# A two-layer encoder step in hi/lo-split fp32: the seven-product pair of token tiles also in layer 0, its passes re-ordered

## The chip, the cores and the metric

The kernel runs on one core of one Trainium2 chip. The metric is device time in microseconds (us) of one execution. Three executions of the kernel before took 2142.72 to 2146.37 us, median 2143.95. One further execution was recorded by the hardware profiler; all rows of the profile come from that one. Engines are called as in the profile: PE (TensorE, matmul), DVE (VectorE), ACT (ScalarE), POOL (GpSimd), SP (SyncE, which issues most DMAs).

## The reference, cut to what matters

1056 token rows (1024 of a prompt, 32 of a running stream), D = 1024 channels, two layers. Each layer is a mixer (layer 0: gated unit; layer 1: pooling over windows of 2, 4, 8 and 16 rows) and an FFN with 4096 hidden channels, with a norm before and behind each, and scales and shifts ("modulation") that come from a condition vector through w_ada.

```
for i in range(DEPTH):                                  # DEPTH = 2
    mod = jax.nn.silu(c) @ w_ada[i] + b_ada[i]
    sh1, sc1, gt1, sh2, sc2, gt2 = jnp.split(mod[:, None, :], N_MOD, axis=-1)
    h = rmsnorm(x, g_norm[i, 0]) * (1 + sc1) + sh1
    ...                                                 # mix: sgu_mixer (i = 0), pool_mixer (i = 1)
    x = x + gt1 * rmsnorm(mix, g_norm[i, 1])
    h = rmsnorm(x, g_norm[i, 2]) * (1 + sc2) + sh2
    f = jnp.square(jax.nn.relu(h @ ffn_w_up[i])) @ ffn_w_down[i]
    x = x + gt2 * rmsnorm(f, g_norm[i, 3])
```

All of it is in fp32. The two FFNs are most of the arithmetic.

## The kernel before, in words

**Tiles and number format.** Channels lie on the 128 partitions, tokens along the free axis. Three token tiles are kept in SBUF throughout: tiles 0 and 1 with 384 columns, tile 2 with 256 prompt and 32 stream columns, 288. `acc[t]` holds a tile's running sum, `hh[t]` and `hl[t]` the normed and modulated input of the next product, split into a high part (fp32r) and the rest. A product of fp32 operands is three matmuls (`products`, L1029 to L1031): high weight by high input, high weight by low input, low weight by high input, for each 128 channels of the contraction. Weights arrive in pieces of 512 KB, 1024 columns; ACT copies the high part (L534 in `do_w`), DVE subtracts it for the low part. All DVE rows of the profile carry L80, the line of the helper that records them, so they are told apart by tile names.

**Slots.** 16 slots of 1024 columns hold split weights, two for a piece. Four of them, the "ring" (tag R), are lent to other uses from a certain point on: when the piece `LEND_AT` is split, `w_call` takes the ring slots out of the turn, and what was the ring becomes room for the block sums below.

**FFN passes.** The FFN of a layer is cut into 8 chunks of 512 hidden channels. A pass is (layer, chunk, tiles): its eight pieces of weights (4 `up`, 4 `dn`) are loaded and split once and used by each of its tiles. The list `passes` (L374 to L381) gives the order on PE and of the weights. Layer 0 before: chunks 0 and 1 of tile 0, of tile 1, of tile 2; chunks 2 and 3 each with all three tiles; then chunks 4 to 7 of tile 0, of tile 1, of tile 2. Layer 1: chunks 0 to 3 of tile 0, of tile 1, then chunks 4 to 7 as pairs (below), then the eight of tile 2.

**A tile's pass** (`ffn_item`, L1453): four `up` products of 8 x 3 matmuls into PSUM (`pf`), ReLU and square on ACT, split into `fh` and `fl`, then `down`: eight products `pg` of 4 x 3 matmuls, each added to `acc` by DVE. `down` is put off (`pending`) and issued by `flush` (L1284) behind the next pass's first `up` product, so that PE has work while the hidden values are split.

**A pair pass** (`pair_item`, L1509, layer 1 chunks 4 to 7 before) takes tiles 0 and 1 at once. The two halves of the contraction (four blocks of 128 each, `HK`), two pieces of weights and two tiles make a 2 x 2 block product, done in seven block products of 12 matmuls where the plain form has eight. For that, DVE sums weight blocks (`quads`, L493, in four steps that take 2, 1, 2 and 2 slots) and sums of the input (`combos`, L1699; block sums `combo[1]` to `combo[4]`; the first of them, which overwrites half of tile 1's `hh` and `hl`, in `first_combo`, L1735). Results are combined by DVE (`r12`, `r22`, `r11`) and copied by ACT (`a1`, `b1`, `a2`, `a3`); the first PSUM tiles are `pfa` and `pfb`, with rows at L1542 to L1544. `paired` (L1919) starts `first_combo` ahead of the first pair pass.

**What sets the order of DVE and ACT work.** Each engine runs its own queue in the order in which the program issues. The program issues PE's work in order of `passes`, and after each product calls `weave` (L806), which advances two things: the stream of weight pieces and w_ada pieces (`stream`, in the order in which they are loaded; `some_ada`, L418 to L424, says how many w_ada pieces go behind a pass's weights, each of which gives DVE multiply-adds `aa`), and the `fillers`, generators that hold a tile's work between mixer and FFN. A filler advances while the program's own count of DVE time is below that of PE time. `finish(tag)` (L817) forces what is left of a filler. `run_ffn` (L1903) forces the filler of a tile ahead of its chunk 0, after a `flush`. `stream_ready` (L707) holds a piece back until its slots are free.

**The fillers around the FFNs.** `mix_to_ffn` (L1666): norm of the mixer's result and residual (`residual`, L916: for each channel block a scalar-tensor-tensor on `acc`, an addition of the kept input `xo_r`), the square sums on PE, then `modulate` (L957) and `apply` (L963): for each block a scalar-tensor-tensor on `acc`, an ACT activation into `hh`, a scalar-tensor-tensor into `hl`. `to_pool` (L1760), behind the last `down` of a tile in layer 0: the same residual, a norm, the pooling windows (`win1p..`), the small products with `pool_w_grp`, then `mix_to_ffn` for layer 1. In layer 1 tile 2's `apply` is kept in `late_norm` and made a filler only within the last pair pass.

Of the kernel before, what the change touches and what calls it, by code (L numbers as in the profile page):

```python
# [9 lines left out]
F32 = mybir.dt.float32  # L10
# [25 lines left out]
def tile_stream_encoder_step(  # L36
# [391 lines left out]
    for _, key, _, _ in [s for s in stream if s[0] == "two"]:  # L428
        for x in ("A1", "A22", "S12", "S34"):
            wpos[("up", key[1], key[2] // 2, x)] = wpos[key]  # L430
# [62 lines left out]
    def quads(n, j, r1, r2):  # L493

        a11, a12, a21, a22 = r1[:, :512], r1[:, 512:], r2[:, :512], r2[:, 512:]
        key = lambda x: ("up", n, j // 2, x)
        s3 = []

        def first():
            s3.append(work.tile([P, 512], F32, tag="aa", bufs=2, name=f"s3_{n}_{j}"))  # L500
            tt(out=s3[0], in0=a11, in1=a21, op=ALU.subtract)
            w_split(key("A1"), r1)

        def second():
            tt(out=a21, in0=a21, in1=a22, op=ALU.add)
            w_split(key("A22"), a22, 512)

        def third():
            tt(out=a22, in0=a21, in1=a11, op=ALU.subtract)
            w_split(key("S12"), r2)  # L510

        def fourth():
            tt(out=a12, in0=a12, in1=a22, op=ALU.subtract)
            state["raw"] -= 1
            wh, wl = w_pair(key("S34"))
            for at, x in ((0, s3[0]), (512, a12)):
                w = slice(at, at + 512)
                act(out=wh[:, w], in_=x, func=AF.Copy)
                tt(out=wl[:, w], in0=x, in1=wh[:, w].bitcast(F32), op=ALU.subtract)
            state["raw"] -= 1  # L520

        subs.extend([(2, first), (1, second), (2, third), (2, fourth)])

# [391 lines left out]

    def residual(st, l, cf, tag, out, store=True, stat=True, loads=None):  # L916
        t = st.t
# [8 lines left out]

        got = []
        yield from st.finish(got)
        r = got[0]
        st2 = Stat(t, tag + "x")  # L930
# [577 lines left out]

    def pair_item(p, after):  # L1509
        l, c, tiles = passes[p]  # L1510
# [45 lines left out]
        def up(jp):  # L1556
            name = f"{l}_{c}_{jp}"
            j = 2 * jp

            def done(key):  # L1560
                w_finish(("up", p, jp, key))

            pa, pb = ps_ms(f"pfa{name}"), ps_up(f"pfb{name}")
            quad_product(pa, jp, ("A1", 0), -11, True)
            a1 = copy(pa, f"a1{name}")
            weave()
            if jp == 0:
                flush()
                finish("combos")
            quad_product(pb, jp, ("S12", 0), 1, True)  # L1570
            b1 = copy(pb, f"b1{name}")
            weave()
            quad_product(pa, jp, ("S12", 512), 2, False)
            done("S12")
            a2 = copy(pa, f"a2{name}")
            weave()
            quad_product(pb, jp, ("S34", 512), -22, False)
            keep(1, j, add(a2, pb, f"r12{name}"))
            weave()
            quad_product(pa, jp, ("S34", 0), 3, False)  # L1580
            done("S34")
            a3 = copy(pa, f"a3{name}")
            keep(1, j + 1, add(a3, b1, f"r22{name}"))
# [4 lines left out]
            keep(0, j, add(a1, pc, f"r11{name}"))  # L1588
            weave()
            quad_product(pa, jp, ("A22", 0), 4, False)  # L1590
            done("A22")
            keep(0, j + 1, t_m(f"r21{name}"), pa[:, :n])
            weave()

        def down():
            sts = {}
            for q in range(4):
                wh, wl = need_w(("dn", p, q))
                for t in reversed(tiles):
                    for d in (2 * q, 2 * q + 1):  # L1600
                        ps = ps_dn(f"pg{l}_{c}_{t}_{d}")
                        terms = []
                        for j in (0, 1, 3, 2) if t == 1 else range(4):
# [9 lines left out]
                        if d % 2 == 1 and t == tiles[0]:  # L1613
                            w_finish(("dn", p, q))
                        weave(d % 2)
            for t in tiles if after is not None else ():
                after(sts[t])

        up(0)
        up(1)  # L1620
        if after is not None:
            fillers.append(late_norm.pop())
# [43 lines left out]
    def mix_to_ffn(st, l):  # L1666
        t = st.t
        out = []
        need_ada(l, 2)
        yield from residual(st, l, 1, f"r1_{l}_{t}", out, store=l == 0 or t < NT - 1)  # L1670
        if l == 1 and t == NT - 1:
# [10 lines left out]

    late_norm = []
    combo = {}
    HK = KB // 2
# [13 lines left out]
    def combos():  # L1699

        while lent["left"]:
            yield 1.0
        units = []
        for tag, n in (("R", 5), ("hh2", 3), ("hl2", 3)):
# [8 lines left out]
        for i in (2, 3, 4):  # L1713
            combo[i] = units[4 * i - 8 : 4 * i - 4]
        combo[1] = [(hh[1][:, k], hl[1][:, k]) for k in range(HK)]
        for k in (0, 2):
            x, y, z = (t_two(f"combo_{v}{k}") for v in "xyz")
            tt(out=x, in0=both(1, k)[0], in1=both(1, k)[1], op=ALU.add)
            tt(out=y, in0=both(1, HK + k)[0], in1=both(1, HK + k)[1], op=ALU.add)
# [4 lines left out]
            tt(out=z, in0=both(0, k)[0], in1=both(0, k)[1], op=ALU.add)  # L1724
            tt(out=x, in0=x, in1=z, op=ALU.subtract)
            yield True
# [3 lines left out]
            tt(out=z, in0=both(0, HK + k)[0], in1=both(0, HK + k)[1], op=ALU.add)  # L1730
            tt(out=z, in0=z, in1=y, op=ALU.subtract)
            keep_parts(z, combo[4][k : k + 2])
            yield False

    def first_combo():  # L1735

        for k in (0, 2):
            x, z = (t_two(f"combo1_{v}{k}") for v in "xz")
            tt(out=x, in0=both(1, k)[0], in1=both(1, k)[1], op=ALU.add)
            tt(out=z, in0=both(0, k)[0], in1=both(0, k)[1], op=ALU.add)  # L1740
            yield True
            tt(out=x, in0=x, in1=z, op=ALU.subtract)
            keep_parts(x, combo[1][k : k + 2])
            yield False
# [158 lines left out]
    def run_ffn(l, after):  # L1903
        for p, (pl, c, tiles) in enumerate(passes):
            if pl != l:
                continue
            if tiles == PAIR:
                if p > 0 and passes[p - 1][2] != PAIR:
                    paired()
                pair_item(p, after if c == 7 else None)  # L1910
                continue
            for t in tiles:
                if c == 0:
                    if any(f[0] == f"ffn{l}_{t}" for f in fillers):
                        flush()
                    finish(f"ffn{l}_{t}")
                ffn_item(p, t, after if c == 7 else None)

    def paired():  # L1919

        def stages():
            yield from first_combo()

        fillers.append(("combos", stages()))

# [157 lines left out]
```

## Time and profile before

| | |
|---|---|
| median of three executions | 2143.95 us (2142.72 to 2146.37) |
| profiled execution, its own time | 2141.37 us |
| its span (first to last instruction) | 2139.6 us |
| PE busy | 99% of the span |
| DVE, ACT, POOL busy | 71%, 48%, 1% |
| DMA | 320 MB moved, 150 GB/s on average |

How to read it: the page gives for each engine the busy time as a share of the span, and the same in 40 slices of 53.5 us each. Matmuls are pipelined and the length of one matmul in the profile includes the overlap with its neighbours, so what PE needs for a stretch is taken from counts over a window, not from the mean length. A group of rows such as `pg L1031` stands for all instructions from one line that write tiles of one name. A wait "A <- B: 1.2" says that the engine stood idle for 1.2 us and that B ended last of what it waited for.

### The profile page before, as it was taken

How to read it: one execution, taken by the hardware profiler on the slowest of the kernel's cores; microseconds unless marked ns; L12 is line 12 of the kernel's file. 1: busy time of each engine (PE TensorE's matmuls, PEld its weight loads, DVE VectorE, ACT ScalarE, POOL GpSimd, SP SyncE). 2: the span in 40 equal slices, each digit the busy share in tenths (PEclk: the TensorE clock that was granted, in tenths of full speed). 3: DMA queues.
4: the chain of work that ended last, by engine and by line, in shares of the span. 5: the costliest groups of instructions: out<-in, count | busy, mean ns of one | idle time of the engine just before them, and what ended most of it. 6: DMA issues, size and time to landing. Idle time of an engine off the chain costs nothing. (4 is left out here: it accounts for less than half of the span.)

```text
span 2139.6 us, 33156 instructions
## 1 busy us (share of the span) xinstructions
PE 2119.9 (99%) x13026; PEld 2054.6 (96%) x13026; DVE 1521.5 (71%) x2688; ACT 1018.0 (48%) x1743; POOL 22.3 (1%) x44
## 2 busy tenths in 40 slices
PE   8999999999999999999999999999999999999998
PEld 6878999999999999999999999999999999999998
DVE  6778838467778548486747879878879854569464
ACT  5634432234456652323445566666555543365454
POOL 0000000000000000000000000000000000001100
PEclk9999999999999999999999999999999999999999
DMA  8586524353447444243645465665545221138672
GB/s 291 163 263 210 182 83 137 94 154 101 138 129 219 128 150 146 86 141 110 191 128 160 145 183 174 188 189 153 175 136 154 83 76 60 59 115 231 171 206 82
DMA packets 401905, 320.18 MB, mean 150 GB/s; under 512 B 47406, under 2 KB 365142, under 8 KB 401748
## 3 DMA queue, kind: packets, MB, share of 16 engines
q1 hardware_dynamic: 400820, 316.77, 48.9%
q8 instruction: 102, 1.67, 0.3%
q0 software_dynamic: 896, 1.28, 0.2%
q14 instruction: 55, 0.45, 0.1%
q10 hardware_dynamic: 32, 0.01, 0.0%
HBM read 287.34 MB, written 30.66 MB: 149 GB/s over the span
## 5 line engine op out<-in xcount | busy, mean ns | idle before, releaser
L1029 PE MATMUL pg<-fh,wh_dn 128*128 128x384 f32 (+1 forms) x1240 | 397.8, 321 | 0.1
L1031 PE MATMUL pg<-fh,wl_dn 128*128 128x384 f32 (+1 forms) x1240 | 395.8, 319 | 1.2 <-DVE wl_dn L80 1.2
L1030 PE MATMUL pg<-fl,wh_dn 128*128 128x384 f32 (+1 forms) x1240 | 396.0, 319 | 0.0
L1029 PE MATMUL pf<-hh,wh_up 128*128 128x384 f32 (+1 forms) x1000 | 318.1, 318 | 0.0
L1031 PE MATMUL pf<-hh,wl_up 128*128 128x384 f32 (+1 forms) x1000 | 316.6, 317 | 0.1
L1030 PE MATMUL pf<-hl,wh_up 128*128 128x384 f32 (+1 forms) x1000 | 316.7, 317 | 0.0
L80 DVE TENSOR_TENSOR acc<-acc,pg 128x384 f32<-128x384 f32 (+1 forms) x336 | 174.1, 519 | 106.5 <-PE pg L1031 105.8
L1029 PEld LDWEIGHTS pg<-fh,wh_dn 128*128 128x128 f32 x1240 | 232.7, 188 | 1.9 <-ACT fh L1289 1.4
L1031 PEld LDWEIGHTS pg<-fh,wl_dn 128*128 128x128 f32 x1240 | 232.7, 188 | 1.4 <-DVE wl_dn L80 1.4
L1030 PEld LDWEIGHTS pg<-fl,wh_dn 128*128 128x128 f32 x1240 | 232.8, 188 | 0.6
L80 DVE TENSOR_TENSOR wl_dn<-raw,wh_dn 128x1024 fp32r<-128x1024 f32 x139 | 170.1, 1224 | 78.4 <-ACT wh_dn L534 67.9
L534 ACT ACTIVATE wh_dn<-raw 128x1024 fp32r<-128x1024 f32 x139 | 146.8, 1058 | 162.9 <-PE pg L1030 122.4
L80 DVE SCALAR_TENSOR_TENSOR aa<-raw,csil,aa 128x512 f32<-128x512 f32 (+1 forms) x364 | 204.5, 623 | 4.9 <-DMA raw<-in_w_ada_dram 4.7
L80 DVE TENSOR_TENSOR wl_up<-raw,wh_up 128x1024 fp32r<-128x1024 f32 x113 | 138.3, 1225 | 76.8 <-ACT wh_up L534 76.6
L1031 PEld LDWEIGHTS pf<-hh,wl_up 128*128 128x128 f32 x1000 | 188.0, 188 | 0.8 <-DVE wl_up L80 0.8
L1029 PEld LDWEIGHTS pf<-hh,wh_up 128*128 128x128 f32 x1000 | 187.6, 188 | 0.6 <-ACT wh_up L534 0.2
L1030 PEld LDWEIGHTS pf<-hl,wh_up 128*128 128x128 f32 x1000 | 187.7, 188 | 0.3
L534 ACT ACTIVATE wh_up<-raw 128x1024 fp32r<-128x1024 f32 x113 | 119.7, 1060 | 115.7 <-PE pf L1030 61.8
L534 ACT ACTIVATE ring<-raw 128x1024 fp32r<-128x1024 f32 x68 | 72.0, 1059 | 154.8 <-PE pf L1030 72.0
L1465 ACT ACTIVATE r<-pf 128x384 f32<-128x384 f32 (+1 forms) x160 | 71.2, 445 | 126.6 <-PE pf L1031 123.8
L80 DVE TENSOR_TENSOR fl<-r,fh 128x384 fp32r<-128x384 f32 (+1 forms) x180 | 93.5, 521 | 50.8 <-ACT fh L1289 50.1
L80 DVE TENSOR_TENSOR ring<-raw,ring 128x1024 fp32r<-128x1024 f32 x69 | 84.2, 1222 | 44.2 <-ACT ring L534 44.2
(403 smaller groups left out, 4555.6 us busy)
## 6 DMA issues: line engine op xcount, KB each, us to landing
raw<-in_ffn_w_up_dram SPq DMA_DIRECT2D x160, 512.0 KB, 4.0
raw<-in_ffn_w_down_dram SPq DMA_DIRECT2D x160, 512.0 KB, 3.5
raw<-in_w_ada_dram SPq DMA_DIRECT2D x92, 512.0 KB, 4.1
raw<-in_sgu_w_in_dram SPq DMA_DIRECT2D x40, 512.0 KB, 4.1
xd<-acc SPq DMA_DIRECT2D x8, 1536.0 KB, 7.2
raw<-in_sgu_w_out_dram SPq DMA_DIRECT2D x24, 512.0 KB, 4.0
xo_r<-xd SPq DMA_DIRECT2D x32, 384.0 KB, 3.5
vd<-vt SPq DMA_DIRECT2D x32, 256.0 KB, 4.5
```

The lines of the kernel that those rows point to most:

```text
L80: return op(out, *args, **kw)
L534: act(out=wh, in_=r, func=AF.Copy)
L1029: mm(ps[:, :n], wh, rh, start=i == 0, stop=False)
L1030: mm(ps[:, :n], wh, rl, start=False, stop=False)
L1031: mm(ps[:, :n], wl, rh, start=False, stop=i == last)
L1465: act(out=r[:, :n], in_=ps[:, :n], func=AF.Relu)
```

## The change

Layer 0's chunks 2 to 5 become pair passes of tiles 0 and 1; tile 2 runs its eight chunks alone behind them. Layer 0's order is now: tile 0 chunks 0, 1, 6, 7; tile 1 chunks 0, 1; the pairs 2 to 5; tile 1 chunks 6, 7; tile 2 chunks 0 to 7. Layer 1's list of passes is as it was. Around this:

- `LEND_AT` is the first FFN piece, so the ring is lent from layer 0 on.
- `some_ada` gives six w_ada pieces to a pair pass in layer 0 and two in layer 1, and two to the single passes of tiles 0 and 1 in layer 0 with a chunk above 1.
- `quads` has three steps of 3, 2 and 2 slots, the weight sums regrouped as S31 and S24; the extra tile `s3` is gone.
- In `pair_item` and `combos` tiles 0 and 1 swap their parts: `combo[1]` overwrites half of tile 0. `first_combo` and `paired` are gone, their work is in `combos`, which waits until tile 1's chunk 0 is entered (`singles`).
- Which tiles end in a pass (`ends`) is worked out from the list; the tile's closing statistics are taken there.
- In layer 0 tile 2's `mix_to_ffn` stops behind the norm's statistics; its residual and modulation are kept in `late_norm`, which is made a filler within the last pair pass, and `combos` is made a filler at that point.

```diff
     every = list(range(NT))
-    passes = [(0, c, [t]) for t in every for c in (0, 1)]
-    passes += [(0, c, every) for c in range(2, 4)]
-    passes += [(0, c, [t]) for t in every for c in range(4, 8)]
     PAIR = every[:2]
+    passes = [(0, c, [0]) for c in (0, 1, 6, 7)]
+    passes += [(0, c, [1]) for c in (0, 1)]
+    passes += [(0, c, PAIR) for c in range(2, 6)]
+    passes += [(0, c, [1]) for c in (6, 7)]
+    passes += [(0, c, [NT - 1]) for c in range(8)]
     passes += [(1, c, [t]) for t in PAIR for c in range(4)]
-    LEND_AT = ("up", len(passes) - 2, 0)
     passes += [(1, c, PAIR) for c in range(4, 8)]
     passes += [(1, c, [NT - 1]) for c in range(8)]
+    LEND_AT = ("up", 0, 0)
...
-        if l == 0:
-            some_ada(12 if len(tiles) > 1 else 4 if c in (4, 5) and tiles == every[:1] else 0)
-        elif tiles == [1]:
+        if tiles == PAIR:
+            some_ada((6, 2)[l])
+        elif l == 0 and c > 1 and len(tiles) == 1 and tiles != [NT - 1]:
             some_ada(2)
...
         def first():
-            s3.append(work.tile([P, 512], F32, tag="aa", bufs=2, name=f"s3_{n}_{j}"))
-            tt(out=s3[0], in0=a11, in1=a21, op=ALU.subtract)
             w_split(key("A1"), r1)
+            w_split(key("A22"), a22, 512)
 
         def second():
-            tt(out=a21, in0=a21, in1=a22, op=ALU.add)
-            w_split(key("A22"), a22, 512)
+            tt(out=a22, in0=a21, in1=a22, op=ALU.add)
+            tt(out=a21, in0=a11, in1=a21, op=ALU.subtract)
+            w_split(key("S31"), r2)
 
         def third():
-            tt(out=a22, in0=a21, in1=a11, op=ALU.subtract)
-            w_split(key("S12"), r2)
-
-        def fourth():
-            tt(out=a12, in0=a12, in1=a22, op=ALU.subtract)
+            tt(out=a11, in0=a22, in1=a11, op=ALU.subtract)
+            tt(out=a12, in0=a12, in1=a11, op=ALU.subtract)
             state["raw"] -= 1
...
+            w_split(key("S24"), r1)
             state["raw"] -= 1
 
-        subs.extend([(2, first), (1, second), (2, third), (2, fourth)])
+        subs.extend([(3, first), (2, second), (2, third)])
...
-        return stream[k][0] not in ("w", "one", "two") or len(slots) >= 2
+        return len(slots) >= {"w": 2, "one": 3, "two": 3}.get(stream[k][0], 0)
...
-    def pair_item(p, after):
+    def pair_item(p, after, ends):
...
-            t, k0 = {-11: (0, 0), -21: (0, HK), -22: (1, HK)}[x]
+            t, k0 = {-11: (1, 0), -21: (1, HK), -22: (0, HK)}[x]
...
-        if after is not None:
+        if passes[p + 1][2] != PAIR:
             fillers.append(late_norm.pop())
         down()
...
         need_ada(l, 2)
+        if l == 0 and t == NT - 1:
+            got = []
+            yield from st.finish(got)
+
+            def rest():
+                yield from residual(st, l, 1, f"r1_{l}_{t}", out, r=got[0])
+                yield from modulate(out[0], l, 2, 3)
+
+            late_norm.append((f"ffn0_{t}", rest()))
+            fillers.append(("combos", combos()))
+            return
         yield from residual(st, l, 1, f"r1_{l}_{t}", out, store=l == 0 or t < NT - 1)
...
     late_norm = []
+    singles = []
...
     def combos():
 
-        while lent["left"]:
+        while lent["left"] or not singles:
             yield 1.0
+        singles.clear()
...
-        combo[1] = [(hh[1][:, k], hl[1][:, k]) for k in range(HK)]
+        combo[1] = [(hh[0][:, k], hl[0][:, k]) for k in range(HK)]
...
-    def first_combo():
...
+            ends = [t for t in tiles if not any(q[0] == l and t in q[2] for q in passes[p + 1 :])]
             if tiles == PAIR:
-                if p > 0 and passes[p - 1][2] != PAIR:
-                    paired()
-                pair_item(p, after if c == 7 else None)
+                pair_item(p, after, ends)
                 continue
             for t in tiles:
                 if c == 0:
                     if any(f[0] == f"ffn{l}_{t}" for f in fillers):
                         flush()
                     finish(f"ffn{l}_{t}")
-                ffn_item(p, t, after if c == 7 else None)
-
-    def paired():
...
+                if tiles == [1] and c == 0:
+                    singles.append(l)
+                ffn_item(p, t, after if t in ends else None)
```

More of the change, by code (lines that the diff above doesn't have):

```diff
@@ L428, in tile_stream_encoder_step @@
     for _, key, _, _ in [s for s in stream if s[0] == "two"]:
-        for x in ("A1", "A22", "S12", "S34"):
+        for x in ("A1", "A22", "S31", "S24"):
             wpos[("up", key[1], key[2] // 2, x)] = wpos[key]
@@ L913, in finish, with residual @@
             yield False
-    def residual(st, l, cf, tag, out, store=True, stat=True, loads=None):
+    def residual(st, l, cf, tag, out, store=True, stat=True, loads=None, r=None):
         t = st.t
@@ L925, in load @@
                 loads.append(i.ins)
-        got = []
-        yield from st.finish(got)
-        r = got[0]
+        if r is None:
+            got = []
+            yield from st.finish(got)
+            r = got[0]
         st2 = Stat(t, tag + "x")
@@ L1598, in down @@
                 wh, wl = need_w(("dn", p, q))
-                for t in reversed(tiles):
+                for t in tiles:
                     for d in (2 * q, 2 * q + 1):
@@ L1602, in down @@
                         terms = []
-                        for j in (0, 1, 3, 2) if t == 1 else range(4):
+                        for j in range(4):
                             o = j * 256 + (d % 2) * P
@@ L1608, in down @@
                         accumulate(t, d, ps, False)
-                        if after is not None:
+                        if t in ends:
                             if d == 0:
@@ L1612, in down @@
                             sts[t].square(d)
-                        if d % 2 == 1 and t == tiles[0]:
+                        if d % 2 == 1 and t == tiles[-1]:
                             w_finish(("dn", p, q))
                         weave(d % 2)
-            for t in tiles if after is not None else ():
+            for t in ends:
                 after(sts[t])
@@ L1620, in pair_item @@
         up(1)
-        if after is not None:
+        if passes[p + 1][2] != PAIR:
             fillers.append(late_norm.pop())
@@ L1669, in mix_to_ffn @@
         need_ada(l, 2)
+        if l == 0 and t == NT - 1:
+            got = []
+            yield from st.finish(got)
+            def rest():
[4 more added lines that the diff above has]
+            return
         yield from residual(st, l, 1, f"r1_{l}_{t}", out, store=l == 0 or t < NT - 1)
@@ L1714, in combos @@
             combo[i] = units[4 * i - 8 : 4 * i - 4]
-        combo[1] = [(hh[1][:, k], hl[1][:, k]) for k in range(HK)]
+        combo[1] = [(hh[0][:, k], hl[0][:, k]) for k in range(HK)]
         for k in (0, 2):
             x, y, z = (t_two(f"combo_{v}{k}") for v in "xyz")
-            tt(out=x, in0=both(1, k)[0], in1=both(1, k)[1], op=ALU.add)
-            tt(out=y, in0=both(1, HK + k)[0], in1=both(1, HK + k)[1], op=ALU.add)
+            tt(out=x, in0=both(0, k)[0], in1=both(0, k)[1], op=ALU.add)
+            tt(out=y, in0=both(0, HK + k)[0], in1=both(0, HK + k)[1], op=ALU.add)
             yield True
@@ L1723, in combos @@
             yield True
-            tt(out=z, in0=both(0, k)[0], in1=both(0, k)[1], op=ALU.add)
+            tt(out=z, in0=both(1, k)[0], in1=both(1, k)[1], op=ALU.add)
             tt(out=x, in0=x, in1=z, op=ALU.subtract)
+            keep_parts(x, combo[1][k : k + 2])
             yield True
@@ L1729, in combos @@
             yield True
-            tt(out=z, in0=both(0, HK + k)[0], in1=both(0, HK + k)[1], op=ALU.add)
+            tt(out=z, in0=both(1, HK + k)[0], in1=both(1, HK + k)[1], op=ALU.add)
             tt(out=z, in0=z, in1=y, op=ALU.subtract)
             keep_parts(z, combo[4][k : k + 2])
-            yield False
-    def first_combo():
[L1737 to L1743, printed above, removed]
             yield False
@@ L1916, in run_ffn @@
                     finish(f"ffn{l}_{t}")
-                ffn_item(p, t, after if c == 7 else None)
-    def paired():
-        def stages():
-            yield from first_combo()
-        fillers.append(("combos", stages()))
+                if tiles == [1] and c == 0:
+                    singles.append(l)
+                ffn_item(p, t, after if t in ends else None)
     run_ffn(0, to_pool)
```

26 lines of the change are left out of this document (10 added, 16 removed).

## The prediction

> **What bounds the kernel now.** I read the page first, then the waits of PE, then the stages by windows.
>
> ```profile
> span 2139.6 us, 33156 instructions
> PE 2119.9 (99%) x13026; PEld 2054.6 (96%) x13026; DVE 1521.5 (71%) x2688; ACT 1018.0 (48%) x1743; POOL 22.3 (1%) x44
> ...
> PE   8999999999999999999999999999999999999998
> DVE  6778838467778548486747879878879854569464
> ```
>
> The reader is to see PE at 99% of the span, slice after slice, and VectorE (DVE) at 71% with many slices at 8 and 9. So time falls only where PE gets less to do, and rises where PE is made to wait. The waits of PE, longest first:
>
> ```profile
> PE xT L687 <- DMA x_rows<-in_x_prompt_dram: 4.2, 1, 4.2
> ...
> PE pfb L1542 <- ACT b L1548: 1.4, 1, 1.4
> PE pg L1031 <- DVE wl_dn L80: 1.2, 1, 1.2
> ...
> PE pf L1031 <- DVE ring L80: 0.8, 1, 0.8
> PE pfb L1543 <- DVE hl L80: 0.7, 1, 0.7
> ```
>
> After the start (4.2 us for x), four waits remain that the change can reach: 1.4 and 0.7 us at the first pair chunk of layer 1, 1.2 us for a wl_dn, 0.8 us for a weight in the ring: 4.1 us. None stands at a tile's entry into an FFN. The stages:
>
> ```profile
> core 0: us, PE busy (x) PEld busy (x) DVE busy (x) ACT busy (x) POOL busy (x), PEclk, DMA share, GB/s
> 1690.00:1740.00 50.00, 50.00 (x288) 49.72 (x287) 28.24 (x44) 18.54 (x34) 0.00 (x0) 1.00 0.19 55
> 1600.00:1650.00 50.00, 50.00 (x290) 49.81 (x289) 48.77 (x71) 26.10 (x44) 0.00 (x0) 1.00 0.57 172
> 1985.00:2015.00 30.00, 30.00 (x226) 29.71 (x225) 13.78 (x22) 14.71 (x23) 3.79 (x7) 1.00 0.78 186
> 2132.00:2136.00 4.00, 0.54 (x5) 0.30 (x4) 3.40 (x8) 1.28 (x4) 2.09 (x2) 1.00 0.33 127
> 2136.00:2139.60 3.60, 0.00 (x0) 0.00 (x0) 0.24 (x1) 0.00 (x0) 0.00 (x0) 0.54 0.53 187
> ```
>
> First row, a stretch inside layer 1's pair chunks: 288 matmuls of 384 columns in 50 us, 0.1736 us each (its length on the page, 0.33 us, includes overlap). Third row, tile 2 with 288 columns: 30 us / 226 = 0.133 us. Second row: VectorE busy for 48.77 of 50 us and PE not idle, so a dense VectorE alone does not stall PE. The last rows come back below.
>
> **Part 1, the products.** Each pair chunk makes its up-projection in 2 x 7 block products of 12 matmuls, 168, where two tiles make 192. Four chunks, 96 matmuls fewer; the order of the built program has exactly 96 fewer rows on PE, all of 384 columns. 96 x 0.1736 = 16.7 us, all on the path, since PE is the bound. Down-projections (192 per pair) and the 20 weight passes of layer 0 stay, and so do the 485 weight and w_ada loads on SP; POOL's queue is the same.
>
> **Part 2, what VectorE gets.** Rows for it, and for the parts behind:
>
> ```profile
> L80 DVE TENSOR_TENSOR wl_dn<-raw,wh_dn 128x1024 fp32r<-128x1024 f32 x139 | 170.1, 1224 | 78.4 <-ACT wh_dn L534 67.9 <-PE pfa L1543 8.9 <-ACT r L1518 1.0
> L80 DVE TENSOR_TENSOR acc<-acc,pg 128x384 f32<-128x384 f32 x224 | 123.7, 553 | 78.5 <-PE pg L1031 78.1
> L80 DVE TENSOR_TENSOR acc<-acc,pg 128x288 f32<-128x288 f32 x112 | 50.4, 452 | 28.0 <-PE pg L1031 27.7
> L80 DVE TENSOR_TENSOR acc<-acc,xo_r 128x768 f32<-128x768 f32 x32 | 30.7, 959 | 0.0
> L80 DVE SCALAR_TENSOR_TENSOR hl<-acc,mod,hh 128x384 fp32r<-128x384 f32 x32 | 18.7, 615 | 0.2 <-ACT hh L989 0.2
> L80 DVE TENSOR_TENSOR raw<-raw,raw 128x512 f32<-128x512 f32 x16 | 11.0, 689 | 0.2
> L80 DVE SCALAR_TENSOR_TENSOR hl<-acc,mod,hh 128x256 fp32r<-128x256 f32 x16 | 7.7, 483 | 0.1
> L80 DVE SCALAR_TENSOR_TENSOR acc<-acc,coef,r_r_2x 128x32 f32<-128x32 f32 x24 | 6.0, 249 | 0.0
> L80 DVE TENSOR_TENSOR combo_z<-hh,hl 128x768 f32<-128x768 f32 x6 | 5.7, 955 | 0.0
> L80 DVE SCALAR_TENSOR_TENSOR aa<-raw,csil,aa 128x512 f32<-128x512 f32 x196 | 135.8, 750 | 1.4 <-DMA raw<-in_w_ada_dram 1.2
> L80 DVE TENSOR_TENSOR r<-a,pfc 128x384 f32<-128x384 f32 x8 | 4.4, 549 | 0.0
> L80 DVE TENSOR_TENSOR win1p<-acc 128x798 f32<-128x798 f32 x4 | 4.0, 996 | 0.0
> L80 DVE SCALAR_TENSOR_TENSOR acc<-win1p,acc 128x768 f32<-128x768 f32 x4 | 3.9, 964 | 0.0
> ```
>
> (partitions x elements, count | busy, mean ns.) The built program has 90 more VectorE instructions: for layer 0's block sums 18 of 768 (0.955) and 16 of 384 (0.55), 26 us; 24 adds of results (0.549), 13 us; 32 sums of weight blocks of 512 (0.689), 22 us; 1.5K more elements to split per two up pieces, 8 x 1.9 = 15 us; less some in layer 1. About 70 us. Cover: a layer-0 pair chunk lasts 360 x 0.1736 = 62.5 us, and its VectorE rows by this table sum to about 52 us, six w_ada items of some 3.6 us in them: 84%, below the 97.5% of the second window. ScalarE gets 56 rows more at 48% share. I cost this at nothing; without that cover each microsecond of VectorE work beyond 62 per chunk would cost one, at most some 5 us a chunk.
>
> The block sums of layer 0 stand in VectorE's queue before the first accumulation of tile 1's chunk 0, two passes before the pair reads them. In layer 1 the sums that the first pair product needs no longer wait for tile 1's last chunk (they overwrite half of tile 0, which is done), so the 1.4 and 0.7 us should go. The 1.2 and 0.8 us hang on one queue position each, which changes; I take them as gone. Together -4.1, between -2 and -4.8. Lending the four ring slots at layer 0's start leaves 12 of 16 for its weights. The windows at 1690 and 1985 ran with 12 and no idle, so nothing; bounds 0 and one wait of 1.2 us.
>
> **Part 3, the re-ordered transitions.** Here lies the cost. Run_ffn, before a tile's chunk 0, flushes the pending down and then forces the rest of that tile's norm and modulation. If the fillers got to it before, that costs nothing. In the kernel before they had:
>
> ```profile
> 718.15 1.21 DVE L80 SCALAR_TENSOR_TENSOR hl<-acc,mod,hh 128x256 fp32r<-128x256 f32 x4
> ```
>
> ```profile
> 743.46 0.29 PE L1029 MATMUL pf<-hh,wh_up 128*128 128x288 f32 x1
> ...
> 1366.00 0.34 PE L1029 MATMUL pf<-hh,ring 128*128 128x384 f32 x1
> ```
>
> ```profile
> L80 DVE SCALAR_TENSOR_TENSOR hl<-acc,mod,hh x8: 612/614/617, 1301.0 to 1316.6; 128x384 fp32r<-128x384 f32 x8
> ```
>
> Tile 2's modulation (16 rows each of acc and hl) ended at 719.4, its first product came at 743.5; tile 0's for layer 1 ended at 1317.2 and was needed at 1366.0. In the changed kernel's order both stand behind the last accumulation of the pass ahead (row numbers of VectorE's queue, repeats marked x):
>
> ```
> 1394 acc1<-acc1,pg0_7_1_7  [waits PE]     last of tile 1, layer 0
> 1400 acc2<-acc2,coef,r_r1_0_2x 128x256    first row of tile 2's modulation
> 1431 hl0_2_2<-acc2,mod,hh0_2_2 128x32     last row of it
> 1680 acc2<-acc2,pg0_7_2_7  [waits PE]     last of layer 0
> 1694 win1p1_0<-acc1 128x2x399             tile 1's pooling in between
> 1700 acc0<-acc0,coef,r_r1_1_0x 128x384    first row of tile 0's modulation, layer 1
> 1707 hl1_2_0<-acc0,mod,hh1_2_0 128x384 x2 last row of it
> ```
>
> PE's queue has, behind each of these last products, only small statistics matmuls and then the entering tile's products, which wait for hh and hl block by block; the first two are interleaved. So PE stalls for the VectorE chain less those two products.
>
> Rows that follow each other start about 0.085 us before the one ahead ends: two of 615 ns and the next start take 1.06 us, four of 483 and 249 take 1.13, and a 1024 one 1.14:
>
> ```profile
> 705.51 1.21 DVE L80 SCALAR_TENSOR_TENSOR acc<-acc,coef,r_r_2x 128x256 f32<-128x256 f32 x4
> 706.64 0.48 DVE L80 SCALAR_TENSOR_TENSOR hl<-acc,mod,hh 128x256 fp32r<-128x256 f32 x1
> ...
> 1499.80 1.15 DVE L80 SCALAR_TENSOR_TENSOR acc<-acc,coef,r_r_1x 128x384 f32<-128x384 f32 x2
> 1500.86 1.22 DVE L80 TENSOR_TENSOR ring<-raw,ring 128x1024 fp32r<-128x1024 f32 x1
> 1502.00 0.62 DVE L80 SCALAR_TENSOR_TENSOR hl<-acc,mod,hh 128x384 fp32r<-128x384 f32 x1
> ```
>
> Layer 1's start, rows 1680 to 1707 with repeats: 4 of 288 (0.37), 5 scalar-tensor-tensors of 384 (0.53), 1 tensor-tensor of 384 (0.47), 3 of 768 (0.875), 1 weight split (1.14), 5 pooling windows (0.91), 2 pooling differences (0.88), 16 rows of modulation (0.53): 1.5 + 2.65 + 0.47 + 2.6 + 1.1 + 4.55 + 1.8 + 8.5 = 23.2 us. With 0.7 us of latencies from PE and ScalarE, 23.9. PE meanwhile can do 38 matmuls, 6.6 us, and 0.6 us of statistics; the other 10 follow the last hl. Stall 16.7 us. Bounds: all 48 matmuls under the chain, 14.2; VectorE 2 us late into the chain, 19.
>
> Tile 2's start, rows 1394 to 1431: 0.47 + 1.14 + 0.47 + 3 x 0.5 = 3.6 us, 1 us for the two ScalarE steps between them, then 8 groups of 1.13 = 9.0 and some 0.6 of waits for hh: 14.2. PE under it: 0.9 of statistics and 43 x 0.133 = 5.7. Stall 7.6 us; bounds 5.1 (no ScalarE waits, all 48 matmuls) and 9.5. Tile 1's start in layer 1 has seven of its eight hl rows within about 4 us of the last accumulation and the eighth within 6.5, under the 8.3 us of the first two products: 0, at most 1.5.
>
> While PE idles its clock may fall: the last two windows have PE's last work at 2132.5 and a granted clock of 0.54 from 2136 on, so idleness of about 4 us halved it once. At layer 1's start PE would be idle some 9 us but for nothing. The 38 matmuls at half clock take 6.6 us more, of which the chain hides most: I take 2 us, between 0 and 6. The Trainium skill, "TensorE: Matmul & The Clock Gate", section "Part 1: The HAM clock gate", says that one idle window of about 3.4 us halves the clock and about 3.4 us of sustained work restores it; the end of this trace agrees, with under 4 us. By that rule the sum would gain an estimated 1.7 us for each such stall, 3.4 for two, against my 2.
>
> Further 0.5 us for the denser VectorE in tile 2's eight chunks.
>
> **The sum.** -16.7 - 4.1 + 16.7 + 7.6 + 2 + 0.5 = +6.0 us. The profiled execution took 2141.37 us (span 2139.6), so 2147.4; it lies 2.6 below the median 2143.95, so 2150.0 against the runs shown.
>
> **The rivals.**
> *The gain stands* (faster). It decides at both entries together: the norms are in time after all, PE never idles there. 2143.95 - 16.7 - 4.1 = 2123. For it: no entry stalled before, with 24 and 49 us of lead. Against it: the queue order, since VectorE cannot reach row 1700 before the accumulation 20 rows ahead, which waits for PE. It wins once the two stalls cost under 16.5 us together. Chance 0.09.
> *Both at their low bounds*: 14.2 + 5.1, no clock loss: 2142.5, not to be told from no change. For it: matmuls go out as blocks arrive. Against: the last block comes last. Chance 0.11.
> *The clock stays half through both modulations*: 38 x 0.1736 + 43 x 0.133 = 12.3 us more instead of 2: 2160. For it: bursts of PE work with pauses between. Against: the pauses inside are under 3 us, and the chain covers part. The Trainium skill, "TensorE: Matmul & The Clock Gate", same section, asks for a sustained busy window, which such bursts may miss. Chance 0.08.
>
> **How the numbers follow.** The forecast, 2150, has 0.72 and its own range 2146 to 2157. A change under 0.2% (4.3 us) can't be told from none here: 2139.7 to 2148.2 counts as the same. Of the forecast's 0.72 some 0.13 lies there, with the low-bound rival 0.24; faster 0.09; slower 0.59 + 0.08 = 0.67. The range 2141 to 2159 leaves out the first rival, most of the third and a few hundredths of tails.
>
> **What would show it.** PE with 96 matmuls fewer; waits of PE pf for hh or hl of several us in all, in two clusters near 1130 and 1350; no PE idle inside layer 0's pair chunks; no pfb wait at layer 1's pair; a granted clock below 1 near 1350. Wrong if PE's busy time falls by 16 us and so does the span, or if PE waits for wl_up or accumulations inside the pair chunks.

## The result and the profile after

The changed kernel took 2162.24 us, the median of four executions (2161.78 to 2164.95); the kernel before, on the same chip, 2143.62. The ratio is 1.0087, with an interval of 1.007 to 1.0105: slower by 18.6 us, where 6 were forecast, and above the range's end of 2159. The profiled execution took 2162.36 us, 21.0 more than the profiled one before. The runs below were taken in two later sessions, in which the kernel before took 2142.61 and 2141.77; so a difference from the changed kernel's 2162 is uncertain by 1 to 2 us, and the ratios to the kernel before are the safer figures. First the page of the changed kernel:

```profile
span 2160.6 us, 33037 instructions
PE 2116.0 (98%) x12930; PEld 2045.1 (95%) x12930; DVE 1580.9 (73%) x2778; ACT 1050.2 (49%) x1801; POOL 22.3 (1%) x44
...
DVE  6778837567788757788886896957969765588564
...
PEclk9999999999999999999999999899999999999999
```

PE has its 96 matmuls less (12930 rows for 13026), VectorE 90 rows and 59 us more, and the slice from 1350 to 1404 us has a granted clock below 0.9 of full speed. The waits of PE in the changed kernel, longest first (total, times, longest):

```profile
PE pn_r_0x L897 <- ACT sc_r_0x L882: 8.8, 1, 8.8
PE pf L1024 <- ACT hh L984: 6.5, 2, 5.1
PE xT L681 <- DMA x_rows<-in_x_prompt_dram: 4.6, 1, 4.6
PE pf L1024 <- ACT wh_up L528: 3.7, 2, 2.0
PE pn_rf L897 <- ACT sc_rf L882: 2.7, 1, 2.7
PE pg L1024 <- ACT wh_dn L528: 2.4, 1, 2.4
PE pg L1025 <- DVE fx L80: 1.8, 6, 0.5
...
PE pg L1024 <- ACT fx L1284: 0.9, 2, 0.4
...
PE pg L1026 <- DVE wl_dn L80: 0.4, 1, 0.4
```

Stages of the changed kernel, and one of the kernel before that answers to the fourth (columns as before):

```profile
1150.00:1175.00 25.00, 19.91 (x122) 18.11 (x121) 18.84 (x46) 17.02 (x39) 0.00 (x0) 0.86 0.31 87
1160.00:1200.00 40.00, 39.09 (x289) 38.40 (x289) 21.49 (x35) 26.74 (x52) 0.00 (x0) 1.00 0.48 139
1370.00:1400.00 30.00, 16.13 (x87) 14.78 (x86) 29.71 (x50) 12.93 (x23) 0.00 (x0) 0.72 0.38 122
2040.00:2100.00 60.00, 55.27 (x392) 54.47 (x391) 33.66 (x44) 28.04 (x42) 0.00 (x0) 0.94 0.64 185
880.00:1070.00 190.00, 189.07 (x1095) 187.14 (x1094) 153.08 (x244) 80.69 (x138) 0.00 (x0) 1.00 0.38 115
```

```profile
2010.00:2070.00 60.00, 58.83 (x436) 57.66 (x435) 36.19 (x48) 31.65 (x49) 0.00 (x0) 1.00 0.70 197
```

The reader is to see four places. At 1150 tile 2 enters layer 0's FFN; behind it, from 1160 to 1200, VectorE is busy for only 21.5 of 40 us. At 1370 tile 0 enters layer 1: VectorE is busy for 29.7 of 30 us and PE runs 87 matmuls. In the 60 us from 2040 PE does 392 matmuls, where the kernel before does 436 in the stretch with its own wait. Inside layer 0's pair chunks (880 to 1070) PE is idle for 0.9 us in 190, with VectorE at 81%.

Added up from the starts of all PE rows (the distance to the next row less the usual distance of its shape), PE lost 41.8 us before and 79.0 after, 37.2 more: tile 2's entry 8.6, tile 0's entry into layer 1 18.0, tile 2's last chunks in layer 1 6.0, layer 0 between 700 and 1150 us 5.0 (most of it one wait for wh_up at 1097), all else -0.4. With -16.6 for the 96 matmuls that is +20.6 of the 21.0.

### The profile page after: what moved, and what is told of

Same layout as the page of the kernel before. It is cut to its first block, busy times and chain, and to the rows that moved or that the text cites. A ratio compares the mean times of both kernels' runs of the same rounds, so it can differ in the third digit from the quotient of the medians.

```text
span 2160.6 us, 33037 instructions
## 1 busy us (share of the span) xinstructions
PE 2116.0 (98%) x12930; PEld 2045.1 (95%) x12930; DVE 1580.9 (73%) x2778; ACT 1050.2 (49%) x1801; POOL 22.3 (1%) x44
## 4 chain that ended last, share of the span: by engine, by line
PE 86%; DVE 6%; DMA 3%; ACT 3%; issue 1%; DVEq 0%; SPq 0%; ACTq 0%
PE pg L1025 10%; PE pg L1026 10%; PE pg L1024 10%; PE pf L1024 7%; PE pf L1025 7%; PE pf L1026 7%; PE po L1024 3%; PE po L1025 3%; PE po L1026 3%; PE pu L1024 3%; PE pu L1026 3%; PE pu L1025 3%; DMA raw<-in_w_ada_dram 2%; PE pv L1050 2%; PE pv L1052 2%; PE pv L1051 2%
## 5 line engine op out<-in xcount | busy, mean ns | idle before, releaser
L1024 PE MATMUL pg<-fh,wh_dn 128*128 128x384 f32 (+1 forms) x1344 | 431.5, 322 | 2.4 <-ACT wh_dn L528 2.4
L1026 PE MATMUL pg<-fh,wl_dn 128*128 128x384 f32 (+1 forms) x1344 | 429.1, 319 | 0.4 <-DVE wl_dn L80 0.4
L1025 PE MATMUL pg<-fl,wh_dn 128*128 128x384 f32 (+1 forms) x1344 | 429.3, 320 | 0.2 <-DVE fl L80 0.2
L528 ACT ACTIVATE wh_dn<-raw 128x1024 fp32r<-128x1024 f32 x160 | 169.1, 1058 | 198.6 <-PE pg L1025 126.8
L80 DVE TENSOR_TENSOR wl_dn<-raw,wh_dn 128x1024 fp32r<-128x1024 f32 x160 | 195.7, 1224 | 83.0 <-ACT wh_dn L528 76.6
L1025 PEld LDWEIGHTS pg<-fl,wh_dn 128*128 128x128 f32 x1344 | 252.7, 188 | 1.6 <-DVE fl L80 0.7
L1026 PEld LDWEIGHTS pg<-fh,wl_dn 128*128 128x128 f32 x1344 | 252.9, 188 | 0.7 <-DVE wl_dn L80 0.7
L80 DVE SCALAR_TENSOR_TENSOR aa<-raw,csil,aa 128x512 f32<-128x512 f32 (+1 forms) x364 | 206.7, 623 | 20.9 <-DMA raw<-in_w_ada_dram 20.9
L1024 PE MATMUL po<-ush,wh_o 128*128 128x384 f32 (+1 forms) x336 | 108.0, 321 | 0.0
L1026 PE MATMUL po<-ush,wl_o 128*128 128x384 f32 (+1 forms) x336 | 107.7, 321 | 0.0
L1025 PE MATMUL po<-usl,wh_o 128*128 128x384 f32 (+1 forms) x336 | 107.7, 320 | 0.0
```

What stands on the lines that cost most here:

```text
L80: return op(out, *args, **kw)
L528: act(out=wh, in_=r, func=AF.Copy)
L1024: mm(ps[:, :n], wh, rh, start=i == 0, stop=False)
L1025: mm(ps[:, :n], wh, rl, start=False, stop=False)
L1026: mm(ps[:, :n], wl, rh, start=False, stop=i == last)
```

## Experiments at the two entries

All are the changed kernel with the edit shown; the times of the kernel before were taken beside them on the same chip.

**The order without the seven products.**

```diff
-                ("one", "two")[j % 2] if tiles == PAIR else "w",
+                ("one", "two")[j % 2] if tiles == PAIR and l == 1 else "w",
...
-    LEND_AT = ("up", 0, 0)
+    LEND_AT = ("up", passes.index((1, 2, [1])), 0)
...
-            if tiles == PAIR:
+            if tiles == PAIR and l == 1:
                 pair_item(p, after, ends)
...
+                if l == 0 and c == 5 and t == 1:
+                    fillers.append(late_norm.pop())
                 ffn_item(p, t, after if t in ends else None)
```

> The order of passes of the changed kernel, the late modulation of tile 2 and its w_ada placement, but the chunks 2 to 5 of layer 0 with eight plain products for tiles 0 and 1 instead of the seven block products; the ring is then lent where it was before, since two plain tiles need all 16 slots. No block sums of layer 0. Theory (VectorE's load by the block sums is what makes both entries late, not the order of passes): tile 2's modulation ends 56 VectorE rows ahead of tile 1's last accumulation and tile 0's 24 rows ahead of layer 0's last, so both stalls (8.7 and 17.9) go and PE has its 96 matmuls back (+16.7 us): 2152, or some 6 less where the weights' wait at the end goes too: 2146 to 2153. Rival (the order of passes alone costs it): the stalls stay, 2179.

Measured: 2146.61 us, ratio 1.0019 (1.0009 to 1.0029) to the 2142.61 of the kernel before. Its page, and the same two stretches:

```profile
PE 2121.4 (99%) x13026; PEld 2055.7 (96%) x13026; DVE 1515.6 (71%) x2674; ACT 1019.4 (48%) x1735; POOL 22.3 (1%) x44
```

```profile
1150.00:1175.00 25.00, 25.00 (x167) 24.52 (x167) 22.51 (x36) 16.23 (x27) 0.00 (x0) 1.00 0.69 210
...
1370.00:1400.00 30.00, 29.55 (x189) 29.32 (x188) 23.54 (x36) 17.59 (x29) 0.00 (x0) 1.00 0.56 170
```

Both stalls are gone: PE is never idle at 1150 and for 0.5 us in 30 at 1370. From layer 0's last matmul to tile 0's first `pg` in layer 1, with the same 120 matmuls of 384 columns between them, this kernel takes 20.9 us and the changed kernel 39.1. So the order of passes alone costs nothing at the entries. What makes tile 2 and tile 0 late is this order together with the block sums: VectorE has 65 us less to do here (1515.6 against 1580.9), and the fillers are served in time. (The ring is lent later in this kernel too, which this run does not separate.) The wait at the end (below) takes 6.6 us here where it took 2.2 in the kernel before: these 4.4 us account for the 4.0 by which the kernel is slower than that one.

**VectorE's list resumed at once after tile 2's entry.**

```diff
                     finish(f"ffn{l}_{t}")
+                    if l == 0 and t == NT - 1:
+                        time["dve"] = min(time["dve"], time["pe"])
```

> The changed kernel with one line more: when tile 2's modulation has been forced ahead of its chunk 0 in layer 0, the program's own count of VectorE time is set back to that of PE, so that fillers are issued again at once. In the changed kernel VectorE was busy for 12.7 and 8.8 us of the 20 us windows from 1160 to 1200, just when tile 0's way into layer 1 was waiting in the list of fillers. Theory (the second stall is in good part made by the first: the forced work leaves the count ahead, and VectorE idle): the order has tile 0's pooling done and the modulation 9 VectorE rows behind the last accumulation of layer 0, where it was 20 rows; by the rows' durations the chain behind that accumulation falls from 23.2 to about 14.5 us, the stall at layer 1's entry from 17.9 to about 8 us, the stall at tile 2's entry stays at about 8.7; time about 2152. Rival (VectorE is simply short of time in tile 2's eight chunks): fillers issued earlier push the weight splits and accumulations back, PE waits for wl_up, wl_dn or pg inside the chunks, and the time stays within 3 us of 2162.

Measured: 2156.33 us (2152.24 to 2156.76), ratio 1.0063 (1.0048 to 1.0078). Stretches and waits:

```profile
1160.00:1200.00 40.00, 38.93 (x275) 37.79 (x276) 33.03 (x62) 27.98 (x57) 0.00 (x0) 0.96 0.60 182
1370.00:1400.00 30.00, 23.48 (x138) 21.87 (x139) 26.39 (x46) 16.25 (x30) 0.00 (x0) 0.89 0.38 118
```

```profile
PE pn_rf L897 <- ACT sc_rf L882: 5.7, 2, 3.0
PE pf L1024 <- ACT wh_up L528: 4.9, 2, 3.4
PE pf L1024 <- ACT hh L984: 4.6, 2, 2.9
...
PE pf L1026 <- DVE wl_up L80: 1.3, 2, 0.9
```

VectorE's gap from 1160 to 1200 is filled (33.0 us busy for 21.5), and from layer 0's last matmul to tile 0's first `pg` 31.0 us pass for 39.1: the entry into layer 1 costs 10 us instead of 18. So part of the second stall was made by the first. But 10 us were expected in all and 6 came. The entry gave 8 of them (3 us of statistics wait (pn_rf) and 3 for hh stayed there, with 6.8 us of half clock). By the sum over PE rows the end gave 2 more; but the wait for wh_up at 1097 was longer in this execution (3.4 us; 3.1 and 3.5 in two others of the same placement, 1.8 in the profile above) and cost 3 more with the half clock behind it, and the denser stretch gave back 1.3 for wl_up. The rival, that the filled gap costs as much elsewhere, is out; the theory is right in kind, and 2 us too generous at the entry.

**w_ada pieces away from tile 1's last two chunks.**

```diff
         if tiles == PAIR:
-            some_ada((6, 2)[l])
-        elif l == 0 and c > 1 and len(tiles) == 1 and tiles != [NT - 1]:
+            some_ada((7, 2)[l])
+        elif l == 0 and c > 1 and tiles == [0]:
             some_ada(2)
```

> The changed kernel with the four w_ada pieces of tile 1's chunks 6 and 7 in layer 0 moved into the four pair passes ahead (seven each instead of six). They are some 14 us of VectorE work (3.6 us each) ahead of tile 2's modulation. Theory (tile 2 enters late because VectorE has too much ahead of its norm in the 67 us of tile 1's last two chunks): five of the sixteen groups' rows come ahead of tile 1's last accumulation and about 8.7 us of VectorE rows stay behind it, of which PE covers 6.6: stall at tile 2's entry about 2 us instead of 8.7; as the fillers behind it start earlier, the modulation of tile 0 for layer 1 begins one row behind layer 0's last accumulation, 10.6 us of rows against 7.2 of cover: about 4 us instead of 17.9. Sum 20 us less: about 2142. Rival (the pair passes are already full on VectorE): with seven pieces PE waits inside them, up to 3.6 us for each of the four, and the time stays at 2155 or more.

Measured: 2141.47 us (2140.22 to 2144.86), ratio 1.000 (0.9991 to 1.001): the loss against the kernel before is gone by moving four pieces of 3.6 us, while the waits at the end stay. The waits:

```profile
PE pf L1025 <- DVE hl L80: 3.0, 6, 0.7
PE pg L1024 <- ACT wh_dn L528: 2.4, 1, 2.4
PE pg L1025 <- DVE fx L80: 2.0, 6, 0.5
...
PE pf L1024 <- ACT wh_up L528: 1.4, 1, 1.4
```

No wait for the statistics (pn_r_0x, pn_rf) is left; the entries show as small waits for hl. By the sum over PE rows tile 2's entry costs 4.4 us, and tile 0's some 5 (25.8 us from layer 0's last matmul to tile 0's first `pg`, where the plain products took 20.9), more than the 2 and 4 expected; the total came out as expected in part because the wait for wh_up at 1097, which I had left in, went too. With seven pieces each the pair passes lost no more than with six: PE was idle for 1.1 us from 880 to 1070, with VectorE at 86%.

**Dummy matmuls against the clock.**

```diff
+    def warm(l, t, n):
+        if (l, t) != (1, 0):
+            return
+        ps = ps_dn(f"warm{n}")
+        for i in range(n):
+            mm(ps[:, :288], onesr, hh[NT - 1][:, i % KB, :], start=i == 0, stop=i == n - 1)
...
+                    warm(l, t, 40)
                     finish(f"ffn{l}_{t}")
+                    warm(l, t, 60)
```

> The changed kernel with 100 added matmuls of 288 columns (0.133 us each) on old data at layer 1's entry, 67 in the gap of 9.0 us ahead of tile 0's statistics and 33 behind it in the gap of 5.4 us; their result is not read. PE is then never idle for more than about 2 us there, and nothing else is changed. Theory (of the 17.9 us at this entry some 2 us are the clock: in the changed kernel half clock was recorded for 17.1 us there, of which PE ran real work for about the last 4.2): no half clock at this place, 2 to 3 us less, 2159 to 2160. Rival 1 (the clock costs nothing, since the products wait for the last hl anyway): 2162. Rival 2 (the half clock runs through the modulation and costs most of a doubled product, 6 us or more): 2156 or less.

Measured: 2163.66 us (2160.39 to 2165.05), ratio 1.0095 (1.0078 to 1.0112), no faster. The stretch of the entry in the changed kernel, and with the added matmuls:

```profile
1376.00:1402.00 26.00, 12.13 (x53) 10.85 (x52) 25.56 (x41) 10.24 (x18) 0.00 (x0) 0.67 0.34 109
```

```profile
1376.00:1402.00 26.00, 24.27 (x163) 23.18 (x162) 25.81 (x43) 10.22 (x19) 0.00 (x0) 1.00 0.39 122
```

The granted clock is 1.00 instead of 0.67 and the time is the same. From layer 0's last matmul to the start of tile 0's first `pg` in layer 1, 120 matmuls of 384 later, the changed kernel took 39.1 us and this one 38.6: the half clock cost 0.5 us. (The time of the whole run would not show it: by the sum over PE rows this execution lost 3.4 us more at 1097 and 2.3 less at the end.) VectorE is busy for 25.6 and 25.8 of the 26 us: its chain sets the end, and slower products hide under it. Rival 1 holds.

## Experiments at the end, and all placements together

In the changed kernel SP's queue before the waits for wh_dn (2051) and wh_up (2081):

```profile
2029.03 13.13 SPq L1941 DMA_DIRECT2D out_dram<-y_sq  x23
2042.25 1.52 SPq L476 DMA_DIRECT2D raw<-in_ffn_w_down_dram  x3
```

**The stores on another queue.**

```diff
-                store_out(1, nc.sync, range(6))
-                store_out(1, nc.gpsimd, range(6, KB))
+                store_out(1, nc.gpsimd, range(KB))
```

> The changed kernel with all 32 output stores of tile 1 on POOL's queue, where 24 of them were on SP's. In the changed kernel 23 stores in a row held SP from 2029.0 to 2042.2, the three wh_dn pieces behind them were issued at 2042.3, and PE waited 2.4 us for wh_dn at 2051 and 2.0 us for wh_up at 2081, each with a half clock of 3.4 us behind it. Theory (the weights are late because their loads stand behind the stores): both waits go, PE's loss from 2040 to 2100 falls from about 8 us to under 1, time about 2156 (2154 to 2158). Rival (the weights are late for want of slots or of DMA bandwidth): the waits stay, time 2160 to 2164.

Measured: 2156.92 us (2155.6 to 2158.86), ratio 1.007 (1.0055 to 1.0085). The same stretch:

```profile
2040.00:2100.00 60.00, 60.00 (x455) 60.00 (x454) 36.41 (x49) 30.86 (x46) 10.71 (x18) 1.00 0.65 190
```

PE does 455 matmuls instead of 392, with no wait. What had made the weights late was their place behind 23 stores of 0.57 us (13.13 / 23) on one queue, not slots, and not the stores' traffic, which is still there.

**The same edit on the kernel before.**

> The kernel before with all 32 output stores of tile 1 on POOL's queue. There the 24 stores held SP from 1994.6 to 2008.5 and PE waited 1.2 us for a wl_dn at 2021. Theory (the weights' wait at the end comes from the stores ahead of the loads on SP, in both kernels): the wait goes, 1 to 2 us less, 2141 to 2142. Rival (in the kernel before, the wait has another cause, its slots): 2142.6, unchanged.

Measured: 2140.35 us, ratio 0.999 (0.9981 to 1.000) to 2141.77. The waits of PE that are left of those quoted in the prediction:

```profile
PE pfb L1542 <- ACT b L1548: 1.4, 1, 1.4
...
PE pfb L1543 <- DVE hl L80: 0.7, 1, 0.7
PE pf L1031 <- DVE ring L80: 0.6, 1, 0.6
```

The 1.2 us for wl_dn are gone. So the wait had this cause in both kernels; by the time alone 1.4 us are at the edge of what these runs can tell.

**All placements together.** Eight w_ada pieces go two each to the last four mixer groups, the pairs of layer 0 get 6, 6, 4 and 4, tile 1's chunks 6 and 7 none, and the stores go on POOL's queue. Nothing is taken out.

```diff
-        if n < 2:
-            some_ada(8)
+        some_ada(8 if n < 2 else 2)
...
         if tiles == PAIR:
-            some_ada((6, 2)[l])
-        elif l == 0 and c > 1 and len(tiles) == 1 and tiles != [NT - 1]:
+            some_ada((6, 6, 4, 4)[c - 2] if l == 0 else 2)
+        elif l == 0 and c > 1 and tiles == [0]:
             some_ada(2)
...
-                store_out(1, nc.sync, range(6))
-                store_out(1, nc.gpsimd, range(6, KB))
+                store_out(1, nc.gpsimd, range(KB))
```

> The changed kernel with two placements moved and nothing taken out: eight w_ada pieces are given to the last four mixer groups' weights (two each), the four pair passes get 6, 6, 4 and 4, tile 1's chunks 6 and 7 get none; and all 32 output stores of tile 1 go on POOL's queue. In the order of VectorE tile 2's modulation then ends 35 rows ahead of tile 1's last accumulation and tile 0's 23 rows ahead of layer 0's last. Theory (the products' gain is real and whole, and what was lost are waits for late fillers and weights): against the changed kernel -8.7 (tile 2's entry), -17.9 (tile 0's), -6 (end), -2 to -4 (wh_up at 1097, whose loads lie beside w_ada pieces that are now elsewhere): 2162 less 35 to 37 = 2125 to 2127, 16 us below the kernel before. Rival (VectorE has not the room: it is busy 73% over all and near 100% in many windows): a new wait comes in the mixer groups or in the pair passes, and the time stays above 2135.

Measured: 2122.99 us (2121.57 to 2124.56), ratio 0.9907 (0.9892 to 0.9922) to the 2141.77 of the kernel before: faster than both, by 18.8 us and, across sessions, 39. Its page and its waits:

```profile
span 2120.6 us, 33027 instructions
PE 2102.3 (99%) x12930; PEld 2038.4 (96%) x12930; DVE 1579.7 (74%) x2778; ACT 1047.0 (49%) x1799; POOL 37.1 (2%) x68
```

```profile
PE xT L680 <- DMA x_rows<-in_x_prompt_dram: 4.5, 1, 4.5
PE pv L1095 <- ACT hh L983: 1.8, 2, 1.1
PE pg L1024 <- DVE fx L80: 1.4, 4, 0.5
PE rowT L218 <- DVE vec L219: 0.9, 1, 0.9
PE pg L1023 <- ACT fx L1283: 0.8, 2, 0.5
```

Behind the first 30 us, in which those for x, hh and vec fall, no wait over 0.5 us is left on PE; VectorE has the same 2778 rows. The gain of the products is whole (16.7) and the end's wait of the kernel before is gone too. The rival, that VectorE has no room, is out: in its mixer stage PE stays busy with the added pieces (199.9 of 200 us from 560 to 760).

## Why the prediction missed

**The products** (-16.7): right. The kernel with all placements took 22.8 us less than the one with plain products (18.8 below the kernel before and 4.0 above it, each in its own session; 23.6 by the plain medians), of which 6.6 are the latter's waits at the end: 16.2 to 17.0 are left for the 96 matmuls.

**The two entries and the clock** (+16.7 + 7.6 + 2 = 26.3): 26.6 measured. The sizes from the order and the durations of rows held: 18.0 for 16.7 at layer 1, 8.6 for 7.6 at tile 2. The clock term was wrong in its own right: at layer 1 it cost 0.5 us, not about 2, since VectorE's chain covers slow products. What made up for it is that each entry cost about 1 us more than its sum; at tile 2's, where the clock was not tried by itself, that 1 us may hold its share. So that the three terms together came out to 0.3 us is luck in part. The Trainium skill's page "TensorE: Matmul & The Clock Gate", section "Part 1: The HAM clock gate", says that an idle window of about 3.4 us halves the clock, and at layer 1's entry, with PE idle for 8.8 and then 5.1 us, it did; the estimate of 1.7 us for each stall that I worked out from it was not paid there. The rival with 12.3 us for the clock is out: the two entries leave no room for it.

**The cause of the entries** was told wrongly: Part 3 put them to the re-ordered transitions, and Part 2 costed VectorE's 70 us of added work (59 measured) "at nothing". Inside layer 0's pair chunks that nearly holds (0.9 us idle in 190). But the plain products in the same order have no stall, so the two entries are where the added work is paid: it pushes the fillers back, and hardly the splits and accumulations of the pair chunks. I had read the late order from the built program without asking what made it late.

**The waits removed** (-4.1) are the step that failed, with "I cost this at nothing" for the rest of Part 2. The 1.4 and 0.7 us at layer 1's first pair and the 0.8 for the ring did go, but as much came back as waits for fx at the down-products of the pairs in both layers (1.8 us in six waits by the list above, and 0.9 more where ACT ended last). In layer 1 VectorE's queue had no multiply-adds of w_ada during the pair chunks before; now it has 36 (23.9 us) there, since `some_ada` gives the pairs two pieces each, and at 1774.6 three of them (2.1 us) stand just ahead of an fx that PE waits for. The 1.2 us for wl_dn I took to hang on a place in VectorE's queue; it hung on SP's, behind the stores. I had compared SP's loads by count (485 both) and not by place against the stores, and in the changed kernel the wait grew to three: 2.4 + 2.0 + 0.4 us and half clock behind the first two, 6.0 more than before. The wait for wh_up at 1097 was not foreseen at all; the chain of waits shows how it comes:

```profile
1083.71 5.06 DMA xo_r<-xd
...
1088.80 0.76 DVE acc L80
...
1091.28 0.88 DVE aa L80 x2
1092.16 1.14 DVE wl_dn L80
...
1093.32 5.41 DMA raw<-in_ffn_w_up_dram
...
1098.75 1.06 ACT wh_up L528
```

Tile 2's residual waits for its kept input in VectorE's queue, the weight split behind it frees its buffer late, and the next load starts late. It went when the w_ada pieces were moved; which of their two effects did it, VectorE's time or the place of their loads, was not separated. So -3.6 was forecast for waits and the denser VectorE, and about +10.6 measured: 14 of the 15 us by which the profiled execution missed its forecast of 2147.4.

## What to carry to other kernels

When an engine off the critical path gets more work, look for its price not where the work is issued but at the next point where something deferred must be ready; here moving other deferrable work ahead was worth more than its length (14 us of w_ada rows moved, about 20 us gained, some 2 of them at the wait at 1097). Compare queues by the place of each transfer against its neighbours, not by counts. A change that saves work and loses time may only lack a better placement of other work: here the same products went from +0.9% to -0.9%.

## What the runs showed of the hardware that was not expected

Waits much shorter than the 4 us that the prediction went by can halve the clock, and the length of the wait alone does not tell whether they do. With 1.97 us of idle PE ahead of wh_up in the changed kernel, and 1.70 us at the same place of the kernel with plain products:

```profile
2083.77 0.40 PE L1024 MATMUL pf<-hh,wh_up 128*128 128x288 f32 x1 [1.97 <-ACT wh_up L528]
```

```profile
2080.00:2090.00 10.00, 8.03 (x49) 7.80 (x48) 4.63 (x6) 5.44 (x10) 0.00 (x0) 0.83 0.82 234
```

```profile
2068.69 0.40 PE L1024 MATMUL pf<-hh,wh_up 128*128 128x288 f32 x1 [1.70 <-ACT wh_up L528]
```

```profile
2066.00:2076.00 10.00, 8.13 (x60) 7.67 (x59) 7.05 (x10) 7.45 (x14) 0.00 (x0) 1.00 0.75 220
```

The first halved the clock for 3.4 us (0.83 over 10 us, and half clock is recorded for 3.4 us), the second did not. The recorded half-clock stretches were all 3.4, 6.8 or 17.1 us, whole multiples of 3.4, but for the one at a run's end. The prediction had taken about 4 us of idleness for it, from the end of the trace; a gap of 2 us is also shorter than the idle window of about 3.4 us that the Trainium skill's page "TensorE: Matmul & The Clock Gate", section "Part 1: The HAM clock gate", gives, while the lengths of the half-clock stretches fit that window. At 1097 a wait of 1.8 us left the clock as it was, and waits of 3.1 to 3.5 us at the same place in three other runs halved it for 3.4 us. But no length between 1.7 and 2 us is a limit: at 16 us into each run PE waits for 1.11 us for hh, with few matmuls around it. In `b_stores` the clock was half for the 3.4 us from 18.0 (PE busy for 1.57 of the 3.40 us ahead), as it was in `e2_ada`; in `e6_early`, with PE busy for 1.58 of the same 3.40 us, it stayed at 1.00, as in the other six runs. What decides there is not shown.
